# A hybrid decoder layer on one core: two lower bounds on GpSimd, a later sum, and other banks round the first scores

## The chip, the core and the metric

The kernel runs on one core of a Trainium2 chip, in one launch. Its time is device microseconds. The engines have names that the profile uses too: PE is TensorE, which multiplies matrices, and PEld is its loading of weights; DVE is VectorE, ACT is ScalarE, POOL is GpSimd, SP is SyncE, which issues most of the DMAs. Tiles of 128 partitions lie in SBUF; PE writes its results to PSUM, which the kernel uses as eight banks of 128x512 fp32.

## The reference, cut to what matters

One layer of a decoder over 1024 tokens of width 1024, all in float32:

```python
u = rms_norm(x, norm1_g)
aq, ak, av, hq, hf, hi, hg = split(u @ w_in)              # seven parts of 512 columns
attn = rms_norm(dilated_attention(aq, ak, av), attn_norm_g)   # 8 heads, windows (128,1) (512,4) (2048,16)
rec = hgrn2_mixer(hq, hf, hi, lb)                             # 4 heads, chunks of 64
rec = rms_norm(rec, hgrn_norm_g) * silu(hg)
h = x + concat(attn, rec) @ w_out
gate, val = split(rms_norm(h, norm2_g) @ w_up)
h = h + (gelu(conv3(gate)) * val) @ w_down
out = rms_norm(h, final_norm_g)

def hgrn2_mixer(q, f, i, lb):
    qf = silu(q)
    forget = lb + (1 - lb) * sigmoid(f)
    ...
```

So the recurrent part needs three kinds of sigmoid: of `hf` for the forget gate, and of `hq` and `hg` for the two silus.

## The kernel before, in words

A projection is done for a pair of 512-column parts at a time, by a scheme of seven products of 2x2 blocks in place of eight (`pair_block`, L527 on). Each operand is split into a high and a low part, so that one 128x128 by 128x512 step of a product is three matmuls (`three`, L514, L515, L516), and a product is four such steps. In a profile row `w<-T2h,whi` is such a matmul: `w` is the PSUM bank of the product, `T2h` the high part of a sum of token blocks, `whi` and `wlo` the parts of a weight block. Weights arrive by SP's DMAs as `raww`, are combined by DVE (L178, L179, L180, L197), cast to `whi` by ACT (L102), and the rest `wlo` is made by DVE (L104). DVE adds the products up out of PSUM (L544 to L556); only the first product of a block is copied out by ACT (L542).

The eight banks are handed out by name: `bank(tag, name)` has the tags "mm", "o", "t" and "s" with two banks each, in turn. Whoever asks for a bank whose turn has come waits until the last reader of its former contents is done. `block_banks[0]` says which tags the products of the next blocks take.

PE's order is written by hand: the program's order of matmuls is the order on PE. Long work (the products of the blocks) is a generator, `fill`, of which a stretch is run between other steps; `fill.run(x)` issues products for about x us. The order on DVE, ACT, POOL and SP is made by a scheduler from the program, so that an edit at one place can move their instructions elsewhere.

The stages that matter here:

- The first block of queries and keys runs before attention begins. After it `block_banks[0]` becomes `cycle(("mm",))` (L733), so that the blocks 1 to 3 take the two "mm" banks in turn, `fill.run(3.9)` issues the first products, and attention begins.
- Attention (L770 to L805) makes for each pair p of heads and block b of queries the scores of two heads into two banks (L788, L790; tags "s","s" for even b, "s","o" for odd b), takes them with mask and minimum to SBUF on DVE (L797), then exp on ACT (L799), reciprocal on DVE (L800), scaling on POOL (L801). Later PE transposes them (L816, L824; tag "t").
- The recurrence and its projections run from about 262 to 470 us. The projected parts are scaled on DVE (L951), bounded from below by -40 and sent through a sigmoid of three ACT instructions (L859, L860, L861): `f_out` (max in L915) for `hf`, `q_out` (L921, product L923) for `hq`, `g_last` (L928, product L930) for `hg`. The generator `recur` (L1015 on) then makes, per head and half of the tokens: two ACT instructions (L1020, L1021), a scan on DVE (L1027), differences and exponentials (L1031 to L1038), transposes on PE (`psK`, L1044), intra-chunk products (`psA`, L1049, L1050), chunk states (`psU`, L1060; L1062 to L1072 on DVE and ACT), a carry copied by POOL (L1075), outputs (`psO`, L1083, L1085, L1092), transposes of these (`psT`, L1098, tag "t"), and the gated result into `G` by DVE (L1100), which sets the "t" bank free.
- Within this stage `attn_stat` (one for each half of the tokens) makes the attention norm's statistic: four loads, squares on ACT (L968), additions on DVE (L970), and, as its second step, a sum over partitions by a matmul with ones into a "t" bank (`ass`, L973) with what follows from it (`rstd_part`, L369 to L373).

When each step of this stage comes is set by a list of times in units of 5.2 us of fill work: `STARTS` and `STAGES_AT` for the recurrence, `STAT = (3.5, 6.8)` plus 0 and 4.0 for the two steps of the statistic. `play` sorts the list and runs `fill` between the steps.

Of the kernel before, what the change touches and what calls it, by code (L numbers as in the profile page):

```python
# [3 lines left out]

# [31 lines left out]
STAT = (3.5, 6.8)  # L36
# [228 lines left out]
def hybrid_kernel(ctx: ExitStack, tc: tile.TileContext, xT, w_qk, w_tok, w_hg, w_out, w_up,  # L265
                  w_down, vecs, amask, hmask, out):
    nc = tc.nc
    PE, DVE, ACT, POOL = nc.tensor, nc.vector, nc.scalar, nc.gpsimd
# [132 lines left out]
    def bank(tag, name):  # L401
        return ps1.tile([P, H2], F32, tag=tag, name=name, bufs=2)
# [19 lines left out]
    def vtile(name):  # L422
        return at.tile([P, H2], F32, tag="vi", name=name, bufs=4)
# [135 lines left out]
    blocks, block_banks = [], [cycle(("mm",))]  # L559
# [136 lines left out]
    for t in TURN:  # L696
        x = vtile(f"it{t}")
        tok_out(ivd, t, x, V[t])

    def run(g):  # L700
        for _ in g:
            pass
# [18 lines left out]
    def qk_block(p):  # L721
        return pair_block(("qk", p), lambda m, hf: mtile(f"u{p}_{m}{hf}"), qk_evac(p))
# [7 lines left out]
    for hf in range(2):  # L730
        rms1_row(hf)
    run(first)
    block_banks[0] = cycle(("mm",))  # L733
    fill.add(*[qk_block(p) for p in range(1, 4)])
    fill.run(3.9)
    xp_cm.__exit__(None, None, None)
# [5 lines left out]
    if True:  # L742
# [29 lines left out]
        def scores(p, b):  # L772

            qp, kp = qk[p]
            far = 32 * max(b - 1, 0)
            near = P if b == 0 else 2 * P
            k0 = (b + 1) * P - near
            n = far + near
            S = [bank(("so" if b % 2 else "ss")[e], f"S{p}_{b}_{e}") for e in range(2)]
            rows = [slice(64 * e, 64 * e + 64) for e in range(2)]  # L780
            k4 = kp.rearrange("p (b r l) -> p r b l", r=4, l=32)
            for part in range(2 if far else 1):
                for r in range(4):
                    o = slice(32 * r, 32 * r + 32)
                    for e in range(2):
                        q = qp[rows[e], b * P + 32 * r : b * P + 32 * r + 32]
                        if part == 0:
                            PE.matmul(S[e][o, far:n], q, kp[rows[e], k0 : k0 + near], start=True, stop=True)  # L788
                        else:
                            PE.matmul(S[e][o, 0:far].rearrange("p (b l) -> p b l", l=32), q,  # L790
                                      k4[rows[e], r, 0 : b - 1], start=True, stop=True)
            m = mask[:, FAR - far :] if b else mask[:, FAR + P :]
            Ps = probs[p, b] = []
            for e in range(2):
                Pt = ab.tile([P, FAR + NEAR], F32, tag=f"P{e}", name=f"P{p}_{b}_{e}", bufs=3)
                st = at.tile([P, 16], F32, tag="st", name=f"st{p}_{b}_{e}", bufs=8)
                DVE.tensor_tensor_reduce(Pt[:, :n], S[e][:, :n], m, -(DH ** -0.5), BIG * 3,  # L797
                                         op0=ALU.add, op1=ALU.min, accum_out=st[:, 0:1])
                ACT.activation(Pt[:, :n], Pt[:, :n], AF.Exp, bias=st[:, 0:1], scale=-1.0, accum_out=st[:, 2:3])  # L799
                DVE.reciprocal(st[:, 3:4], st[:, 2:3])  # L800
                POOL.tensor_scalar(Pt[:, :n], Pt[:, :n], st[:, 3:4], 1.0, op0=ALU.mult, op1=ALU.mult)  # L801
                Ps.append(Pt)
# [55 lines left out]
        def sigmoid(dst, src):  # L858
            ACT.activation(dst, src, AF.Exp, scale=-1.0)  # L859
            ACT.activation(dst, dst, AF.Ln, bias=1.0)  # L860
            ACT.activation(dst, dst, AF.Exp, scale=-1.0)  # L861
# [17 lines left out]
        for x in slots[:LAG]:  # L879
            scores(*x)  # L880
            fill.run(1.5)
        ends = []
        for n, (p, b) in enumerate(slots):
            if n + LAG < len(slots):
                scores(*slots[n + LAG])
            if b == 0:
                for kb in range(2):
                    load_values(p, kb)
            fill.run((1.0 if ends else 2.5) if n < 22 else (0.8 if ends else 1.8))
            while ends:  # L890
                values(*ends.pop())
            turn(p, b)
            if b % 4 == 3:
                ends.append((p, b // 4))
# [6 lines left out]
    with pool("hg", "right") as hg:  # L901
# [3 lines left out]
        def ht(tag, nm, bufs=1):  # L905
            return hg.tile([P, H2], F32, tag=tag, name=nm, bufs=bufs)
# [3 lines left out]
        def tile_of(kind, h, hf):  # L910
            tag, bufs = {"hf": ("A", 4), "hq": ("E", 5), "hg": ("GH"[h // 2], 4)}[kind]
            return ht(tag, f"{tag}{h}_{hf}", bufs)
# [5 lines left out]

        def q_out(h, hf, E):
            F = ht("F", f"F{h}_{hf}")  # L920
            DVE.tensor_scalar_max(F, E, -40.0)  # L921
            sigmoid(F, F)
            DVE.tensor_mul(E, E, F)  # L923
            gate.setdefault((h, hf), {}).update(E=E)

        def g_last(h, hf, g_):
            F = ht("F", f"Fg{h}_{hf}")
            DVE.tensor_scalar_max(F, g_, -40.0)  # L928
            sigmoid(F, F)
            DVE.tensor_mul(g_, g_, F)  # L930
            G[h, hf] = g_
# [3 lines left out]
        def g_out(h, hf, g_):  # L935
            if (h, hf) in ready:
                g_last(h, hf, g_)
            else:
                waiting[h, hf] = g_

        def g_now(h, hf):
            ready.add((h, hf))
            if (h, hf) in waiting:
                g_last(h, hf, waiting.pop((h, hf)))

        OUT = {"hf": f_out, "hq": q_out, "hg": g_out}

        def hg_block(pair):
# [14 lines left out]
        def attn_stat(hf):  # L963
            acc = ht("H", f"asq{hf}", 4)
            for c in range(4):
                x = ar[c % 2]
                nc.sync.dma_start(x, rawd[c, hf])
                ACT.activation(x if c else acc, x, AF.Square)  # L968
                if c:
                    DVE.tensor_add(acc, acc, x)  # L970
            yield
            ss = bank("t", f"ass{hf}")
            PE.matmul(ss, ones, acc, start=True, stop=True)  # L973
            R2.append(rstd_part(ht("R", f"R2_{hf}", 2), acc, ss, 1.0 / 512))
            yield

        def attn_parts(hf):
            hi, lo = spare(f"attn{hf}")
            for c in range(4):
                a = ring.raw(rawd[c, hf])  # L980
                DVE.scalar_tensor_tensor(a, a, col(V_AG + c), R2[hf], op0=ALU.mult, op1=ALU.mult)
                ACT.copy(hi[:, c], a)
                DVE.tensor_sub(lo[:, c], a, f32(hi[:, c]))
            return hi, lo
# [16 lines left out]
        for hf in range(2):  # L1001
            for kind, h in HG[0]:
                x = tile_of(kind, h, hf)
# [121 lines left out]
        steps = []  # L1125
# [16 lines left out]
            steps += zip((start, *(start + x for x in STAGES_AT)), rec_steps(h, hf))  # L1142
        for hf in range(2):
            stat = attn_stat(hf)
            steps += [(STAT[hf] + x, lambda stat=stat: next(stat, None)) for x in (0, 4.0)]
            steps.append((PARTS[hf], lambda hf=hf: attn_ops.update({hf: attn_parts(hf)})))
        steps.sort(key=lambda x: x[0])
        done = 0
# [548 lines left out]
```

## Time and profile before

| | |
|---|---|
| median of 3 runs | 1142.49 us (1142.37 to 1142.78) |
| profiled execution, its time | 1142.57 us |
| its span, first to last instruction | 1140.6 us |
| mean granted TensorE clock | 0.998 |
| DVE, ACT, POOL busy | 85%, 51%, 8% of the span |
| PE busy from 268 to 316 us | 47.09 of 48 us |
| DVE busy from 268 to 316 us | 44.99 of 48 us |
| DVE busy from 390 to 470 us | 60.93 of 80 us |

A row of a timeline gives the start in us from the span's beginning, the duration in us, engine, line and operation, out<-in by the program's names, shapes, and the number of instructions put together; in brackets stands the time for which the engine was idle just before, and what ended that. Durations of neighbours on one engine overlap, so that the step from start to start is shorter than a duration. In a row of groups the count is followed by busy time in us, the mean in ns, and the idle time ahead of them with its releasers. In the view of waits a row is: who waited, for which producer, us in total, times, the longest. A row of windows has the busy time of each engine in a stretch, with the number of instructions in brackets.

### The profile page before, as it was taken

The page shows a single profiled execution, that of the slowest core. Times are in us where ns is not written, and L with a number is a line of the kernel's source. Part 1 is how long each engine was busy: PE and PEld are TensorE (multiplying, and loading weights), DVE is VectorE, ACT ScalarE, POOL GpSimd, SP SyncE. Part 2 cuts the span into 40 slices and gives each one's busy share as a digit, 9 for nine tenths or more (in the row PEclk, how much of TensorE's full clock was granted, in tenths as well). Part 3 has the DMA queues.
Part 4 walks back from the last instruction along what each step waited for, and adds up shares of the span by engine and source line. Part 5 has one row for each costly group of instructions (what it writes and reads, how often), then busy time and mean ns, then how long its engine had stood idle before and what let it go on. Part 6 is the DMA issues. An engine that isn't in the chain of part 4 may idle for free.

```text
span 1140.6 us, 17940 instructions
## 1 busy us (share of the span) xinstructions
PE 1127.5 (99%) x6404; PEld 927.4 (81%) x6404; DVE 970.2 (85%) x1768; ACT 580.6 (51%) x1151; POOL 89.9 (8%) x107
## 2 busy tenths in 40 slices
PE   9999999999999999999999999999999999999996
PEld 8888677778878888888788888888888888888885
DVE  7687977778999985989999999888988789857987
ACT  7545545465788665564433434343434444444553
POOL 5200333330000002000000000000000000000000
PEclk9999999999999999999999999999999999999999
DMA  7147322224315542311233223322332376435532
GB/s 251 64 169 235 73 71 62 85 76 159 102 57 179 168 139 92 104 50 56 65 121 111 92 103 120 117 79 100 120 117 79 134 263 219 120 94 176 157 120 74
DMA packets 102088, 136.13 MB, mean 119 GB/s; under 512 B 25392, under 2 KB 44624, under 8 KB 102000
## 3 DMA queue, kind: packets, MB, share of 16 engines
q1 hardware_dynamic: 87712, 110.33, 31.6%
q10 hardware_dynamic: 14288, 24.67, 5.8%
q8 instruction: 50, 0.82, 0.3%
q14 instruction: 38, 0.31, 0.1%
HBM read 100.20 MB, written 34.76 MB: 118 GB/s over the span
## 4 chain that ended last, share of the span: by engine, by line
PE 93%; DVE 5%; DMA 1%; issue 1%; ACT 0%; DVEq 0%; ACTq 0%
PE p L1298 11%; PE p L1297 11%; PE p L1296 11%; PE w L514 5%; PE w L515 4%; PE w L516 4%; PE ds L1595 3%; PE ds L1597 3%; PE ds L1596 3%; PE po L514 3%; PE po L516 3%; PE po L515 3%; PE da L1597 2%; PE da L1595 2%; PE da L1596 2%; PE S L788 2%
## 5 line engine op out<-in xcount | busy, mean ns | idle before, releaser
L102 ACT CAST whi<-raww 128x512 fp32r<-128x512 f32 x253 | 154.5, 618 | 209.3 <-PE p L1297 75.4
L104 DVE TENSOR_TENSOR wlo<-raww,whi 128x512 fp32r<-128x512 f32 x254 | 176.9, 699 | 23.1 <-ACT whi L102 21.5
L102 ACT CAST whi<-r 128x512 fp32r<-128x512 f32 x70 | 43.6, 623 | 82.6 <-PE ds L1596 46.2
L104 DVE TENSOR_TENSOR wlo<-r,whi 128x512 fp32r<-128x512 f32 x70 | 48.0, 687 | 18.9 <-ACT whi L102 18.9
L1596 PE MATMUL ds<-flo,whi 128*128 128x512 f32 x160 | 62.3, 389 | 0.0
L1595 PE MATMUL ds<-fhi,whi 128*128 128x512 f32 x160 | 62.2, 389 | 0.0
L1296 PE MATMUL p<-b1h,whi 128*128 128x512 f32 x160 | 62.2, 389 | 0.0
L1297 PE MATMUL p<-b1l,whi 128*128 128x512 f32 x160 | 62.2, 389 | 0.0
L1298 PE MATMUL p<-b1h,wlo 128*128 128x512 f32 x160 | 62.2, 389 | 0.0
L1597 PE MATMUL ds<-fhi,wlo 128*128 128x512 f32 x160 | 62.2, 389 | 0.0
L801 POOL TENSOR_SCALAR P<-P,st 128x128 f32<-128x128 f32 (+7 forms) x64 | 47.1, 742 | 97.2 <-DVE st L800 77.1
L1569 POOL TENSOR_TENSOR facc<-facc,sqf 128x256 f32<-128x256 f32 x2 | 1.5, 735 | 670.9 <-ACT sqf L1568 670.9
L104 DVE TENSOR_TENSOR flo<-rawf,fhi 128x512 fp32r<-128x512 f32 x70 | 48.1, 687 | 4.0 <-ACT fhi L102 4.0
L102 ACT CAST fhi<-rawf 128x512 fp32r<-128x512 f32 x70 | 43.1, 616 | 13.2 <-PE p L1298 5.0
L1325 ACT ACTIVATE cv<-cv 128x512 f32<-128x512 f32 x44 | 27.8, 633 | 41.6 <-DVE cv L1318 41.6
L799 ACT ACTIVATE P<-P,st 128x128 f32<-128x128 f32 (+7 forms) x64 | 35.7, 559 | 25.6 <-DVE st L797 25.6
L1318 DVE SCALAR_TENSOR_TENSOR cv<-g,vec,cv 128x511 f32<-128x511 f32 (+2 forms) x92 | 44.8, 492 | 3.4 <-ACT cv L1315 3.1
L1595 PE MATMUL da<-fhi,whi 128*128 128x512 f32 x120 | 46.7, 389 | 0.0
L1596 PE MATMUL da<-flo,whi 128*128 128x512 f32 x120 | 46.7, 389 | 0.0
L1597 PE MATMUL da<-fhi,wlo 128*128 128x512 f32 x120 | 46.7, 389 | 0.0
L797 DVE CUSTOM_DVE_ANT_0 P<-S,mask 128x128 f32<-128x128 f32 (+7 forms) x64 | 28.8, 486 | 8.7 <-PE S L790 6.6
L1597 PEld LDWEIGHTS ds<-fhi,wlo 128*128 128x128 f32 x160 | 30.0, 188 | 6.3
(589 smaller groups left out, 3411.3 us busy)
## 6 DMA issues: line engine op xcount, KB each, us to landing
raww<-in_w_up_dram SPq DMA_DIRECT2D x88, 256.0 KB, 2.9
rawf<-spT SPq DMA_DIRECT2D x40, 256.0 KB, 2.8
r<-in_w_down_dram SPq DMA_DIRECT2D x40, 256.0 KB, 3.5
spB<-a ACTq DMA_DIRECT2D x30, 256.0 KB, 2.2
spT<-t ACTq DMA_DIRECT2D x30, 256.0 KB, 2.1
rawf<-spB SPq DMA_DIRECT2D x30, 256.0 KB, 2.8
raww<-in_w_out_dram SPq DMA_DIRECT2D x28, 256.0 KB, 2.8
raww<-in_w_hg_dram SPq DMA_DIRECT2D x24, 256.0 KB, 2.8
```

Of the source, the lines that this page charges most:

```text
L102: self.pin(self.high(hi[:, :w], raw))
L104: self.pin(low.tensor_sub(lo[:, :w], raw, f32(hi[:, :w])))
L514: PE.matmul(ps, a[0], b[0], start=start, stop=False)
L515: PE.matmul(ps, a[0], b[1], start=False, stop=False)
L516: PE.matmul(ps, a[1], b[0], start=False, stop=stop)
L801: POOL.tensor_scalar(Pt[:, :n], Pt[:, :n], st[:, 3:4], 1.0, op0=ALU.mult, op1=ALU.mult)
L1296: PE.matmul(ps, hi[:, s], bhi, start=(start and n == 0), stop=False)
L1297: PE.matmul(ps, hi[:, s], blo, start=False, stop=False)
L1298: PE.matmul(ps, lo[:, s], bhi, start=False, stop=(stop and n == len(rhs) - 1))
L1595: PE.matmul(ps[d], hi[:, s], ahi, start=(k == 0), stop=False)
L1596: PE.matmul(ps[d], hi[:, s], alo, start=False, stop=False)
L1597: PE.matmul(ps[d], lo[:, s], ahi, start=False, stop=(k == NPAIR - 1))
```

## The change

Four edits:

1. The first two products of the second query and key block take the two "t" banks, those behind them "mm" in turn as before.
2. The scores of pair 0, block 0, take the tags "s" and "t" in place of "s" and "s".
3. The max with -40 in `q_out` and in `g_last` is issued on POOL in place of DVE: six and eight instructions of 128x512. That of `f_out` stays on DVE.
4. The second step of `attn_stat` is asked for at +4.3 in place of +4.0 units, that is 0.3 x 5.2 = 1.56 us of fill work later, in both halves.

```diff
-from itertools import cycle
+from itertools import chain, cycle
...
     run(first)
-    block_banks[0] = cycle(("mm",))
+    block_banks[0] = chain(('t', 't'), cycle(("mm",)))
     fill.add(*[qk_block(p) for p in range(1, 4)])
     fill.run(3.9)
...
-            S = [bank(("so" if b % 2 else "ss")[e], f"S{p}_{b}_{e}") for e in range(2)]
+            S = [bank(("so" if b % 2 else "ss" if (p, b) != (0, 0) else 'st')[e], f"S{p}_{b}_{e}") for e in range(2)]
...
         def q_out(h, hf, E):
             F = ht("F", f"F{h}_{hf}")
-            DVE.tensor_scalar_max(F, E, -40.0)
+            POOL.tensor_scalar_max(F, E, -40.0)
             sigmoid(F, F)
             DVE.tensor_mul(E, E, F)
...
         def g_last(h, hf, g_):
             F = ht("F", f"Fg{h}_{hf}")
-            DVE.tensor_scalar_max(F, g_, -40.0)
+            POOL.tensor_scalar_max(F, g_, -40.0)
             sigmoid(F, F)
             DVE.tensor_mul(g_, g_, F)
...
             stat = attn_stat(hf)
-            steps += [(STAT[hf] + x, lambda stat=stat: next(stat, None)) for x in (0, 4.0)]
+            steps += [(STAT[hf] + x, lambda stat=stat: next(stat, None)) for x in (0, 4.3)]
```

What it does to the order is shown at three places; in these rows a number behind a name tells one tile from the next of that name, and + is the kernel with the change.

First, DVE at the first scores: `S_0_0`, `S_0_1` are the two heads' scores of block 0, `S_1_0` the first of block 1, `u_01` the block's sum.

```order
 L197 TENSOR_TENSOR raww_1111<-raww_1111,raww_1057 128x512
 L544 TENSOR_TENSOR u_01_1178<-u_00_1159,w_1179 128x512
+L104 TENSOR_TENSOR wlo_1245<-raww_1111,whi_1244 128x512
 L797 ISA P_0_0_1228,st_0_0_1229<-S_0_0_1218,mask 128x128
 L797 ISA st_0_0_1229 128x1
 L797 ISA P_0_1_1234,st_0_1_1235<-S_0_1_1219,mask 128x128
 L797 ISA st_0_1_1235 128x1
-L104 TENSOR_TENSOR wlo_1245<-raww_1111,whi_1244 128x512
-L800 RECIPROCAL st_0_0_1229<-st_0_0_1229 128x1
-L800 RECIPROCAL st_0_1_1235<-st_0_1_1235 128x1
 L797 ISA P_1_0_1263,st_1_0_1264<-S_1_0_1253,mask 128x256
```

The rest of a weight block, L104, now stands ahead of the scores' first two reads, and the two reciprocals between them and block 1's read stand behind it. PE's order is the same here as before.

Second, PE at the first statistic's sum, taken from the place where it stood to the one where it stands.

```order
 L516 MATMUL w_3862<-T2h,wlo_3699 128x512
 L1060 MATMUL psU_1_3866<-iv_1_3642,kT_1_3790 128x128 x3
-L973 MATMUL ass_3880<-asq_3573,ones 128x512
 L514 MATMUL w_3862<-T2h,whi_3698 128x512
 L515 MATMUL w_3862<-T2l,whi_3698 128x512
```

```order
 L515 MATMUL w_3862<-T2l,whi_3698 128x512
 L516 MATMUL w_3862<-T2h,wlo_3699 128x512
+L973 MATMUL ass_3902<-asq_3573,ones 128x512
 L514 MATMUL w_3862<-T2h,whi_3698 128x512
 L515 MATMUL w_3862<-T2l,whi_3698 128x512
```

It stands two steps of a product, six matmuls, later. On DVE the instruction that sets its bank free, L1100, stands in these rows:

```order
 L104 TENSOR_TENSOR wlo_3827<-raww_3694,whi_3826 128x512
-L923 TENSOR_TENSOR E_1_3703<-E_1_3703,F_1_3753 128x512
 L556 TENSOR_TENSOR A_1_3599<-w_3801,A_1_3599 128x512
-L921 TENSOR_SCALAR F_0_3795<-E_0_3680 128x512
+L1100 SCALAR_TENSOR_TENSOR G_0_3387<-psT_0_3844,vec,G_0_3387 128x512
 L951 TENSOR_TENSOR A_1_3599<-A_1_3599,R_90 128x512
-L1100 SCALAR_TENSOR_TENSOR G_0_3387<-psT_0_3844,vec,G_0_3387 128x512
+L1027 SCALAR_TENSOR_TENSOR C_0_3885<-chunks,A_0_3551 128x512
+L923 TENSOR_TENSOR E_0_3680<-E_0_3680,F_0_3795 128x512
 L915 TENSOR_SCALAR A_1_3599<-A_1_3599 128x512
```

L1100 has moved ahead of one L951. The scan L1027, which stood just ahead of the first of these rows before, stands behind it. A max of `q_out` is gone from between; one L923 has moved a few rows up, and a few rows ahead of all these an L197 is new that stood behind L1100 before.

Third, ACT at the first max that is now on POOL: `Fg_0` is its result, the input of the first sigmoid of `g_last`.

```order
 L102 CAST whi_3445<-raww_3439 128x512
 L1021 ACTIVATE A_0_3372<-A_0_3372,lb 128x512
+L859 ACTIVATE Fg_0_3714<-Fg_0_3714 128x512
 L1033 ACTIVATE ex_0_3466<-C_0_3464 128x4
 L1034 ACTIVATE ex_0_3466<-C_0_3464 128x4
 L102 CAST whi_3485<-raww_3439 128x512
+L860 ACTIVATE Fg_0_3714<-Fg_0_3714 128x512
 L1032 ACTIVATE ex_0_3466<-A_0_3372 128x4
```

The three instructions of this sigmoid stood about 25 places further back; two of them are now ahead of the recurrence's exponentials and of a weight cast.

## The prediction

> **What bounds the kernel now.** I read the page first, then what PE waited for, then PE's timeline at each of these waits, and last the timelines of VectorE (DVE), ScalarE (ACT) and GpSimd (POOL) round the same moments. The first two rows are the head of the page and its list of busy times.
>
> ```profile
> span 1140.6 us, 17940 instructions
> ...
> PE 1127.5 (99%) x6404; PEld 927.4 (81%) x6404; DVE 970.2 (85%) x1768; ACT 580.6 (51%) x1151; POOL 89.9 (8%) x107
> ```
>
> TensorE is busy 1127.5 of 1140.6 us, so PE's idle time is the whole stock from which a change of waits can draw: 13.1 us. The view of PE's waits says how little of it lies in the middle.
>
> ```profile
> PE warm L433 <- DVE eps L295: 1.1, 1, 1.1
> PE w L514 <- ACT u L542: 1.0, 1, 1.0
> PE ass L973 <- DVE G L1100: 0.9, 1, 0.9
> PE S L788 <- DVE st L797: 0.5, 1, 0.5
> ```
>
> The first is the start, which the diff doesn't touch. The other three, each met once, sum to 2.4 us; the remaining 9.6 us are start and tail, untouched too. Each of the three belongs to an edit: `w` to the new banks of the block, `S` to the bank of the first scores, `ass` to the later sum. The gain is thus a little under 3 us at the most. A difference of 0.2%, 2.28 us, is about what a measurement of this kernel can tell from no change, so full success is just over that bound and two thirds of it is not.
>
> **Edit 1, banks of the block.** PE's timeline at the first wait:
>
> ```profile
> 117.53 0.39 PE L516 MATMUL w<-B11h,wlo 128*128 128x512 f32 x1
> 118.93 0.50 PE L514 MATMUL w<-T2h,whi 128*128 128x512 f32 x1 [1.01 <-ACT u L542]
> 119.26 0.40 PE L515 MATMUL w<-T2l,whi 128*128 128x512 f32 x1
> 119.50 0.39 PE L516 MATMUL w<-T2h,wlo 128*128 128x512 f32 x1
> ```
>
> The second product of the block (T2) reuses the "mm" bank of the first, which ACT has copied out when PE goes on at 118.93. From start to start that is 1.40 us where the last two rows step by 0.24: 1.16 too many; and the step behind it, 0.33, is 0.09 too long: **1.25 us**. With a "t" bank for each of the two, the wait for that copy is gone. The copy now stands in the way of whoever takes the first bank next, the second half of scores (0,0), which edit 2 gives a "t" bank. By the order PE gets there after nine matmuls of T2, 9 x 0.24 = 2.2 us from 117.77: at 119.9, 1.0 us after the copy's end. So nothing is passed on, and the term lies between 1.0 (the wait alone) and 1.25.
>
> **Edit 2, bank of the first scores.** PE at the second wait, and the next scores, which do not wait:
>
> ```profile
> 122.83 0.40 PE L516 MATMUL w<-B21h,wlo 128*128 128x512 f32 x1
> 123.68 0.67 PE L788 MATMUL S<-kp,qp 64*32 64x256 f32 x16 [0.46 <-DVE st L797]
> ...
> 125.54 0.40 PE L516 MATMUL w<-B21h,wlo 128*128 128x512 f32 x1
> 125.87 0.66 PE L788 MATMUL S<-kp,qp 64*32 64x256 f32 x16
> ```
>
> Scores take 0.85 us after a matmul in the first case and 0.33 in the second: **0.52 us**. Late next are the third scores, (0,2), which need both "s" banks: one is free early, the other must be read by L797 of (0,1). DVE now:
>
> ```profile
> 122.64 0.69 DVE L544 TENSOR_TENSOR u<-u,w 128x512 f32<-128x512 f32 x1 [0.56 <-PE w L516]
> 123.24 0.28 DVE L797 CUSTOM_DVE_ANT_0 P<-S,mask 128x128 f32<-128x128 f32 x1
> ...
> 124.56 0.41 DVE L797 CUSTOM_DVE_ANT_0 P<-S,mask 128x256 f32<-128x256 f32 x1
> ```
>
> L544 waited 0.56 us, so DVE's L197 ahead of it was done at 122.08; its product comes 1.25 us earlier now, so it follows L197 at once. The new order puts L104 ahead of the scores' L797. L104's weight cast on ACT needs L197's result, so it begins at 122.08 too and lasts as long as L104 or a little less, by estimate 0.65 with the handing over: L104 starts near 122.75, and L797 of (0,0) 0.60 later (as from 122.64 to 123.24), near 123.35. With two of these at 0.2 (0.28 less the overlap of rows, 122.64 + 0.69 - 123.24 = 0.09), the first of (0,1) begins at 123.75 and ends at 124.16. PE is at the third scores at 125.87 - 1.25 - 0.52 = 124.10. With a release of 0.1 it waits about **0.2 us**; nothing if the cast comes earlier, 0.5 to 0.7 if DVE is late by half an L104 or more.
>
> **Edit 4, the later sum.** PE at the third wait:
>
> ```profile
> 314.01 0.83 PE L1060 MATMUL psU<-iv,kT 128*128 128x128 f32 x6
> 315.75 1.13 PE L973 MATMUL ass<-asq,ones 128*128 128x512 f32 x2 [0.91 <-DVE G L1100]
> ```
>
> The sum's "t" bank was the last transposes', and L1100 reads it late. The wait is 0.91 us, and by the excess of the other two over their waits (1.25 against 1.01, 0.52 against 0.46) it costs 0.97 to 1.15: I take **1.1 us**. PE now does six more matmuls first, 6 x 0.24 = 1.4 us, so it is at the sum at 314.84 + 1.4 = 316.2 where before it was at 314.84 (315.75 less 0.91). DVE is read in the rows behind this paragraph. By the last of them L1100 in the old pace ends at 315.69, half a microsecond before that. Both engines come earlier by the first two terms: DVE waited for PE at the first of these rows and moves with it until then.
>
> ```profile
> 274.52 0.69 DVE L545 TENSOR_TENSOR G<-w,G 128x512 f32<-128x512 f32 x1 [0.72 <-PE w L516]
> ...
> 276.40 1.22 DVE L1027 TENSOR_TENSOR_SCAN C<-chunks,A 128x512 f32<-128x512 f32 x1
> ...
> 278.72 0.69 DVE L548 TENSOR_TENSOR G<-w,G 128x512 f32<-128x512 f32 x1
> ...
> 314.95 0.74 DVE L1100 SCALAR_TENSOR_TENSOR G<-psT,vec,G 128x512 f32<-128x512 f32 x1
> ```
>
> By the order of the changed kernel L1100 also stands ahead of the next scan (1.22 less the overlap, 1.13) and of one L951 (0.6, as any of this size), and behind one L197 (0.6) more. With the three maxes that leave DVE ahead of it (0.34 each, next paragraph) DVE has 1.13 + 0.6 - 0.6 + 1.0 = 2.1 us less to do before it. The cover is 0.5 + 2.1 = 2.6 us. The statistic's later readers cost nothing: the second sum stands six matmuls later as well, and PE doesn't wait there now. The sum's loads and squares stay at their step; no DMA is moved.
>
> **Edit 3, two kinds of max on POOL.** The groups of DVE, in the window from 262 to 462 us, that leave it (14 in all, four more read `H`), and in the next fence the nearest thing that POOL does:
>
> ```profile
> L921 DVE TENSOR_SCALAR F<-E 128x512 f32<-128x512 f32 x6 | 2.5, 418 | 0.0
> L928 DVE TENSOR_SCALAR Fg<-G 128x512 f32<-128x512 f32 x4 | 1.7, 422 | 0.0
> ```
>
> ```profile
> L801 POOL TENSOR_SCALAR P<-P,st 128x448 f32<-128x448 f32 x8 | 6.4, 801 | 9.3 <-DVE st L800 9.3
> ```
>
> DVE steps about 0.34 us at such a max (0.42 less the overlap): 14 x 0.34 = 4.8 us less on DVE. POOL has room: its own time, by estimate at most 0.8 x 512/448 = 0.9 us each, waits included, falls into a stage where it does next to nothing (a row under the rivals). What isn't free is how the two engines get at memory. The carry's copy on POOL, in a full and in a quiet stretch of DVE, then the DVE row at which the first one got through, and one of DVE from the kernel's start:
>
> ```profile
> 298.86 2.76 POOL L1075 COPY carry<-U 128x128 f32<-128x128 f32 x1 [42.68 <-PE w L516]
> ```
>
> ```profile
> 408.08 0.29 POOL L1075 COPY carry<-U 128x128 f32<-128x128 f32 x1 [18.79 <-DVE U L1071]
> ```
>
> ```profile
> 301.39 0.68 DVE L548 TENSOR_TENSOR E<-w,A 128x512 f32<-128x512 f32 x1
> ```
>
> ```profile
> 23.12 1.78 DVE L104 TENSOR_TENSOR wlo<-raww,whi 128x512 fp32r<-128x512 f32 x1
> ```
>
> The same copy takes 0.29 us in the quiet and 2.76 while DVE runs back to back on SBUF tiles; it ends at 301.62, 0.23 us after DVE begins L548, which reads a bank of PSUM. Conversely, that L104, between POOL's long additions at the start, takes 1.78 us, not the 0.69 of the other DVE rows of this size. So a max on POOL waits for a gap, up to 2.5 us, and its user on ACT waits with it; DVE's price per max lies between -0.34 (nothing held) and 1.78 - 0.69 - 0.34 = +0.75 us. I take the end near -0.34, since POOL got in beside L548 there, and that L548 kept its 0.68. The Trainium skill ("SBUF — State Buffer", section "Who interferes with whom") says that a GpSimd instruction reading SBUF and a DVE instruction with two SBUF inputs lock each other out for whole instructions, the first issued winning; the copy's 2.76 against 0.29 agrees. By that rule a lucky order costs DVE nothing and an unlucky one a max's length each, which is the slower rival below.
>
> The added wait matters where something is queued behind it. ACT now has the first sigmoid of `Fg0_0` ahead of this row:
>
> ```profile
> 277.66 0.21 ACT L1033 ACTIVATE ex<-C 128x4 f32<-128x4 f32 x1 [1.78 <-DVE C L1027]
> ```
>
> The max's input is ready as the scan of 276.40 begins. If it gets in at once it ends near 277.3 and the sigmoid (0.6) ends before 277.9, 0.2 late. If it waits for the first DVE instruction that reads PSUM, the L548 of 278.72 above, it ends near 279.4, and ACT is 2.3 us late. Behind it stand a weight cast and the recurrence's exponentials, for which DVE's L104 and L1037, L1038 wait, for these PE:
>
> ```profile
> 281.14 0.68 DVE L1038 TENSOR_TENSOR B<-B,A 128x512 f32<-128x512 f32 x1
> ```
>
> ```profile
> 285.89 0.60 PE L1044 MATMUL psK<-ident,B 128*128 128x128 f32 x4
> ```
>
> PE has 285.89 - 281.82 = 4.1 us of cover there, and the sum above 2.6. Without that cover the hold would cost its 2.3 us whole. So edit 3 by itself is **0** for PE, whose waits in the stage are none but `ass`; its relief of DVE is of use to the sum alone.
>
> **The sum.** 1.25 + 0.52 - 0.2 + 1.1 = 2.7 us. The profiled execution took 1142.57 us (span 1140.6 and 2.0 around it), 0.1 above the median of 1142.49; 1142.57 - 2.7 = 1139.9, and I give that for the median too.
>
> **Rivals.** *The sum still waits.* POOL's waits make L1100 late by more than the cover: a hold of 2.3 us, and three maxes that hold DVE by 0.1 or more each. For it: DVE in the stage that follows is as full as this row shows (columns PE, PEld, DVE, ACT, POOL busy, clock, DMA share, GB/s).
>
> ```profile
> 316.00:390.00 74.00, 74.00 (x404) 61.32 (x404) 73.20 (x136) 59.17 (x143) 2.08 (x2) 1.00 0.42 129
> ```
>
> Against it: that the order takes 2.1 us out ahead of L1100. It keeps 0.5 to 0.9 of the 1.1: 1140.6.
>
> *The score stall only moves.* The third scores wait 0.5 to 0.7, since the cast ahead of L104 is later than I have it: 1140.3. For it: the cast's 0.65 is an estimate, and PE is there 0.1 us ahead of its bank as it is. Against it: every step of DVE there is counted with the new order's instructions, and L197, on which the cast hangs, had no wait of its own to move.
>
> *Slower.* POOL's maxes hold DVE as in the row of 23.12. Ten of the fourteen, the groups quoted, stand before 390 us, where DVE has 0.8 us of idle in 74. At +0.75 each, 7.5 us, and with ACT's 2.3, DVE is 9.8 us late; PE's cover of 4.1 is used up and 5.7 us come out as waits at the recurrence's matmuls: 1139.9 + 5.7 = 1145.6. It decides as soon as DVE's lateness passes 4 us, about five maxes in. Against it: a max is one pass of 0.6 to 0.9 us, not POOL's train of long additions, and most gaps are at instructions that read PSUM.
>
> *The change does not do what it says.* The block's new banks could free nothing if the scores then waited for them; the order shows the bank of each, and it has 1.1 us of room. More than 2.9 us would need a wait elsewhere to go.
>
> **How the numbers follow.** Forecast 0.58 (1139.3 to 1140.2), the sum still waits 0.17, the scores' stall moves 0.12, slower 0.07, both middle rivals or little gain 0.04, more gain 0.02. The first ends at 1140.2, which is the bound for faster: 0.60 with the last. The two middle rivals and the mixed case end between 1140.3 and 1142: 0.33 within 0.2%. The range, 1139.3 to 1142.0, leaves out the slower rival and the two fringes.
>
> **What would show it.** In the profile after, PE's view of waits should have lost L514 behind L542 and L973 behind L1100, and may have a new S L788 behind L797 of about 0.2. POOL's L921 and L928 should last 0.6 to 2.8 us each, and DVE's rows next to them should keep their 0.68 (1.3 or more would be the slower rival). L1100 should end before PE reaches the sum. The prediction is wrong if PE shows a wait at psK, psU or psT between 268 and 390 us, or if a wait appears at a place that I have not named.

## The result, and the profile after

| | before | after |
|---|---|---|
| median | 1142.67 us (1142.37 to 1142.86, 5 runs) | 1150.38 us (1148.71 to 1151.33, 5 runs) |
| ratio, 95% interval | | 1.0065 (1.0055 to 1.0076) |
| profiled execution, span | 1142.57, 1140.6 us | 1150.2, 1148.4 us |

The kernel became slower by 0.65%, 7.7 us, where 2.7 us of gain were forecast. The head of the page of the changed kernel and its view of PE's waits:

```profile
span 1148.4 us, 17955 instructions
...
PE 1130.7 (98%) x6404; PEld 928.7 (81%) x6404; DVE 969.2 (84%) x1754; ACT 579.7 (50%) x1151; POOL 112.6 (10%) x121
```

```profile
PE po L514 <- DVE h L1191: 3.2, 1, 3.2
PE w L514 <- DVE A L544: 1.4, 1, 1.4
PE psO L1085 <- ACT st L1072: 1.3, 3, 0.6
PE psT L1098 <- DVE on L1092: 1.1, 2, 0.6
PE warm L433 <- DVE eps L295: 1.0, 1, 1.0
```

The three waits of before are all gone, and 7.0 us of others stand in their place. PE's busy time also rose by 3.2 us for the same 6404 matmuls. Where each lies is told by the starts of the same PE instruction in both traces:

| PE instruction | before | after | difference |
|---|---|---|---|
| first product, at the start | 6.74 | 7.23 | +0.49 |
| first T2 matmul of the block | 118.93 | 118.17 | -0.76 |
| scores (0,1) | 123.68 | 122.27 | -1.41 |
| L515 of the T2 product behind the first sum | 318.33 | 315.75 | -2.58 |
| psO, second half's carry | 346.39 | 346.61 | +0.22 |
| first T1 matmul, L514 | 350.70 | 352.67 | +1.97 |
| psT | 378.25 | 381.13 | +2.88 |
| first po matmul of attn1 | 397.19 | 403.45 | +6.26 |
| the seventh behind it | 398.80 | 406.61 | +7.81 |

The gains came as forecast, and more: 1.25 and 0.65 at the first two places, then 1.17, 3.1 us in all by 318 us. Behind that 10.4 us are lost until 407 us, and nothing more to the end. PE's timeline of the changed kernel at the block's banks, at the scores and at the sum, which answer to the three stalls of before:

```profile
117.95 0.39 PE L516 MATMUL w<-B11h,wlo 128*128 128x512 f32 x1
118.17 0.39 PE L514 MATMUL w<-T2h,whi 128*128 128x512 f32 x1
...
121.94 0.40 PE L516 MATMUL w<-B21h,wlo 128*128 128x512 f32 x1
122.27 0.66 PE L788 MATMUL S<-kp,qp 64*32 64x256 f32 x16
...
124.12 0.40 PE L516 MATMUL w<-B21h,wlo 128*128 128x512 f32 x1
124.45 0.45 PE L788 MATMUL S<-kp,qp 64*32 64x256 f32 x8
```

```profile
314.42 0.40 PE L516 MATMUL w<-T2h,wlo 128*128 128x512 f32 x1
314.66 1.02 PE L973 MATMUL ass<-asq,ones 128*128 128x512 f32 x2
```

None of the three waits: T2 starts 0.22 us behind the matmul ahead of it, both scores 0.33, the sum 0.24. Then the loss. POOL's groups, and what ACT and DVE waited for from 268 to 412 us:

```profile
L921 POOL TENSOR_SCALAR F<-E 128x512 f32<-128x512 f32 x6 | 10.4, 1728 | 46.0 <-DVE E L951 20.1 <-ACT A L861 12.2 <-DVE hss L373 7.8
L928 POOL TENSOR_SCALAR Fg<-H 128x512 f32<-128x512 f32 x4 | 8.2, 2052 | 20.0 <-DVE H L930 10.5 <-DVE hss L373 9.5
...
L928 POOL TENSOR_SCALAR Fg<-G 128x512 f32<-128x512 f32 x4 | 6.9, 1725 | 29.5 <-DMA raww<-in_w_hg_dram 20.5 <-DVE E L923 8.9
```

```profile
ACT Fg L859 <- POOL Fg L928: 13.1, 6, 3.6
ACT F L859 <- POOL F L921: 11.9, 6, 3.8
```

```profile
DVE wlo L104 <- ACT whi L102: 6.4, 5, 2.6
DVE E L923 <- ACT F L861: 4.6, 5, 1.3
```

On the mean of a group a max lasts 1.7 to 2.1 us on POOL (single ones 1.48 to 3.00) where it lasted 0.42 on DVE, and ACT stood still for POOL twelve times, 25.0 us in all. Before, it had waited for these maxes on DVE six times, 7.7 us. What stands behind on ACT is late too, and so is DVE, which waited 11.0 us in these two rows: for the products behind the sigmoids (L923), and for weight casts that have nothing to do with a sigmoid but stand behind one on ACT (L104; 2.8 us there before).

The largest wait shows the whole chain. POOL, ACT, DVE and PE of the changed kernel, each from its timeline:

```profile
397.81 3.00 POOL L928 TENSOR_SCALAR Fg<-H 128x512 f32<-128x512 f32 x1 [3.01 <-DVE H L930]
```

```profile
400.84 0.63 ACT L859 ACTIVATE Fg<-Fg 128x512 f32<-128x512 f32 x1 [3.62 <-POOL Fg L928]
401.38 0.19 ACT L370 ACTIVATE hss<-hss 128x4 f32<-128x4 f32 x1
401.47 0.60 ACT L102 CAST whi<-raww 128x512 fp32r<-128x512 f32 x1
```

```profile
397.57 1.29 DVE L1111 TENSOR_TENSOR rec0l<-G,rec0h 128x512 fp32r<-128x512 f32 x2
398.78 0.69 DVE L1111 TENSOR_TENSOR rec1l<-G,rec1h 128x512 fp32r<-128x512 f32 x1
402.11 0.69 DVE L104 TENSOR_TENSOR wlo<-raww,whi 128x512 fp32r<-128x512 f32 x1 [2.64 <-ACT whi L102]
402.71 0.68 DVE L1191 TENSOR_TENSOR h<-po,xr 128x512 f32<-128x512 f32 x1
```

```profile
403.45 0.79 PE L514 MATMUL po<-attn1h,whi 128*128 128x512 f32 x1 [3.19 <-DVE h L1191]
404.05 0.63 PE L515 MATMUL po<-attn1l,whi 128*128 128x512 f32 x1
404.47 0.63 PE L516 MATMUL po<-attn1h,wlo 128*128 128x512 f32 x1
```

The max, issued while DVE runs three L1111 on SBUF tiles, takes 3.00 us. ACT waits 3.62 us for it with a weight cast two rows behind, DVE 2.64 for that cast, and PE 3.19 for L1191, which stands on DVE behind L104 and empties PE's bank. The weight cast, L104, L1191 and the matmul all wait in line behind the sigmoid, and none of them uses its result.

### The profile page after: what moved, and what is told of

It reads as the page before. It is cut to its first block, busy times and chain, and to the rows that moved or that the text cites. A ratio compares the mean times of both kernels' runs of the same rounds, so it can differ in the third digit from the quotient of the medians.

```text
span 1148.4 us, 17955 instructions
## 1 busy us (share of the span) xinstructions
PE 1130.7 (98%) x6404; PEld 928.7 (81%) x6404; DVE 969.2 (84%) x1754; ACT 579.7 (50%) x1151; POOL 112.6 (10%) x121
## 4 chain that ended last, share of the span: by engine, by line
PE 89%; DVE 5%; ACT 2%; POOL 1%; issue 1%; DMA 0%; SPq 0%; DVEq 0%; POOLq 0%
PE p L1298 11%; PE p L1296 11%; PE p L1297 11%; PE w L514 5%; PE w L516 4%; PE w L515 4%; PE ds L1597 3%; PE ds L1596 3%; PE ds L1595 3%; PE po L514 2%; PE da L1597 2%; PE da L1596 2%; PE da L1595 2%; PE po L516 2%; PE po L515 2%; PE S L788 2%
## 5 line engine op out<-in xcount | busy, mean ns | idle before, releaser
L104 DVE TENSOR_TENSOR wlo<-raww,whi 128x512 fp32r<-128x512 f32 x254 | 178.1, 704 | 27.7 <-ACT whi L102 26.1
L104 DVE TENSOR_TENSOR wlo<-r,whi 128x512 fp32r<-128x512 f32 x70 | 48.1, 688 | 19.5 <-ACT whi L102 18.6
L801 POOL TENSOR_SCALAR P<-P,st 128x128 f32<-128x128 f32 (+7 forms) x64 | 46.3, 728 | 95.6 <-DVE st L800 90.3
L104 DVE TENSOR_TENSOR flo<-rawf,fhi 128x512 fp32r<-128x512 f32 x70 | 48.0, 686 | 3.7 <-ACT fhi L102 3.7
L1596 PEld LDWEIGHTS ds<-flo,whi 128*128 128x128 f32 x160 | 30.0, 188 | 6.3
L1298 PEld LDWEIGHTS p<-b1h,wlo 128*128 128x128 f32 x160 | 30.0, 188 | 6.3
```

Of the source, the lines that this page charges most:

```text
L104: self.pin(low.tensor_sub(lo[:, :w], raw, f32(hi[:, :w])))
L1298: PE.matmul(ps, lo[:, s], bhi, start=False, stop=(stop and n == len(rhs) - 1))
L1596: PE.matmul(ps[d], hi[:, s], alo, start=False, stop=False)
```

## The experiments

Three theories stood against each other. *Latency*: a max lasts so much longer on POOL that ACT, which takes its instructions in order, waits for it, and DVE for ACT. *Ports*: POOL and DVE stop each other at SBUF, as the slower rival had it. *Order*: the rearranged rows on DVE and ACT are late by themselves. All times are medians; the kernel before had 1142.5 to 1142.9 us beside them.

**Which edit.** Edit 3 left out (`no_pool`), and edit 3 alone (`pool_only`):

```diff
-            POOL.tensor_scalar_max(F, E, -40.0)
+            DVE.tensor_scalar_max(F, E, -40.0)
...
-            POOL.tensor_scalar_max(F, g_, -40.0)
+            DVE.tensor_scalar_max(F, g_, -40.0)
```

> Edits 1, 2 and 4 without the maxes on POOL. In the trace of the change PE's starts gained 1.25 us at the block's banks, 0.66 at the scores and 1.2 at the sum against the kernel before, and lost some 10.5 us behind those, so far put down to the maxes. Theory 'latency' (a max on POOL lasts 1.5 to 3 us, ACT waits for it in order, DVE for ACT) and theory 'ports' (POOL and DVE stop each other at SBUF) both expect 1139.3 to 1140.0 us here and no PE wait behind 130 us. Theory 'order' (the edits' rearranging of DVE and ACT makes the waits, whoever runs the max) expects more than 1143.

Measured: 1140.56 us (1140.24 to 1141.32), ratio 0.9981 (0.9972 to 0.9990). The loss is gone; that leaves out theory *order* as it was put. But the time is 0.6 above what was expected, and PE does wait behind 130 us (the traced execution took 1141.32 us, the longest of the eleven):

```profile
PE w L514 <- DVE A L544: 0.8, 1, 0.8
PE ass L973 <- DVE G L1100: 0.3, 1, 0.3
```

> Edit 3 alone on the kernel before. Theories 'latency' and 'ports' expect the loss whole: 1142.6 + 10.5 = 1153 us, a little less if the statistic's sum hides some of it, 1150 to 1154. Theory 'order' (all edits together) expects 1142 to 1146.

```diff
-            DVE.tensor_scalar_max(F, E, -40.0)
+            POOL.tensor_scalar_max(F, E, -40.0)
...
-            DVE.tensor_scalar_max(F, g_, -40.0)
+            POOL.tensor_scalar_max(F, g_, -40.0)
```

Measured: 1152.58 us (1151.64 to 1153.06), ratio 1.0085 (1.0071 to 1.0099). Edit 3 by itself costs 9.9 us.

**How long the max is, and whom it holds.** A small kernel with POOL and DVE alone:

```python
for _ in range(4): POOL.tensor_scalar_max(a, a, -40.0)                                    # L78, nothing beside it
...
for _ in range(4): POOL.tensor_scalar(a, a, st[:, 3:4], 1.0, op0=ALU.mult, op1=ALU.mult)  # L82
...
for _ in range(4): POOL.tensor_scalar_mul(a, a, 1.0)                                      # L88
...
POOL.tensor_copy(e, a)                                                                    # L90
...
for _ in range(14): DVE.tensor_add(c, c, d)     # L101, both inputs in SBUF; beside it four maxes, L103
...
for _ in range(14): DVE.tensor_add(c, c, w)     # L110, w in PSUM; beside it four maxes, L112
```

> Only a few instructions: POOL's max of 128x512 alone, four times in a row, and other forms of the same size; then DVE additions on SBUF tiles back to back with four maxes beside them, the same with one input in PSUM, and with one in three so. The rest of the layer is left out. Theory 'latency' expects a lone max of about 1.5 us (the shortest in the trace of the change was 1.48) and DVE additions that keep their step of 0.60 beside it. Theory 'ports' expects a lone max of 0.6 to 0.9 us, and additions on SBUF that step by 1.1 or more beside it.

Its POOL and DVE timelines (L80 is the max with a multiplication behind it in one instruction):

```profile
3.38 6.19 POOL L78 TENSOR_SCALAR a<-a 128x512 f32<-128x512 f32 x4 [2.96 <-DMA a<-in_xT_dram]
9.65 7.93 POOL L80 TENSOR_SCALAR a<-a 128x512 f32<-128x512 f32 x4
17.68 3.05 POOL L82 TENSOR_SCALAR a<-a,st 128x512 f32<-128x512 f32 x4
...
31.60 6.20 POOL L88 TENSOR_SCALAR a<-a 128x512 f32<-128x512 f32 x4
37.86 0.61 POOL L90 COPY e<-a 128x512 f32<-128x512 f32 x1
44.37 7.21 POOL L103 TENSOR_SCALAR f<-f 128x512 f32<-128x512 f32 x4 [5.90 <-DVE c L99]
57.93 6.18 POOL L112 TENSOR_SCALAR g<-g 128x512 f32<-128x512 f32 x4 [6.36 <-DVE c L108]
```

```profile
44.32 11.29 DVE L101 TENSOR_TENSOR c<-c,d 128x512 f32<-128x512 f32 x14
...
57.88 10.07 DVE L110 TENSOR_TENSOR c<-c,w 128x512 f32<-128x512 f32 x14
```

A lone max lasts 6.19/4 = 1.55 us, 3.7 times the 0.42 that it took on DVE in the kernel before. The form of instruction from which the prediction sized it, L801's two multiplications, takes 3.05/4 = 0.76 on a tile of the same size, so columns alone don't give the price. Nor is the max dear as such: one multiplication by a number, L88, also lasts 1.55. What in the form makes the difference, these rows don't say. Beside additions on SBUF a max lasts 1.80 and DVE loses (11.29 - 10.07)/4 = 0.3 us per max; beside additions with an input in PSUM neither loses anything (with one in three so, a max lasts 1.64). Theory *latency* had the max right; its step of 0.60 for DVE's additions was not met, since these step by 0.72 where nothing is lost and by 0.81 beside the maxes on SBUF. Theory *ports* missed both: it had 0.6 to 0.9 for the lone max and 1.1 or more for the step. So the ports are real, but not as dear for DVE as 0.75 us a max. For POOL they can be: the max of 3.00 us above, beside three L1111 with their inputs in SBUF, is 1.45 us longer than a lone one.

**The same order, another length.** Here only POOL's operation is another; the rows on DVE and ACT are those of the change.

```diff
-            POOL.tensor_scalar_max(F, E, -40.0)
+            POOL.tensor_copy(F, E)
```

and the same for `g_` (`copy_len`), or

```diff
-            POOL.tensor_scalar_max(F, E, -40.0)
+            POOL.tensor_scalar(F, E, -40.0, 1.0, op0=ALU.max, op1=ALU.mult)
```

(`slow_len`).

> The whole change, with POOL's 14 maxes replaced by copies of the same tiles: the lower bound is left out, the order on DVE and ACT is that of the change, row for row. A lone POOL copy took 0.61 us beside 1.55 for the lone max. Theory 'latency': each max on the path is 0.94 shorter, and with 7 to 10 of them on the path 6.5 to 9.5 of the 10.5 us come back: 1141 to 1144 us. Theory 'ports': at most what DVE lost beside the maxes in the small kernel, (11.29 - 10.07)/4 = 0.3 us each, 14 x 0.3 = 4.2 us: 1146 or more. Theory 'order' (these rows in this order are late whatever the max lasts): 1150.

Measured: 1141.53 us (1140.94 to 1142.02), ratio 0.9990 (0.9981 to 0.9999).

> The whole change, with the max followed by a multiplication by one in the same POOL instruction: 1.98 us alone in place of 1.55, the same order on DVE and ACT, and the same result. Theory 'latency': 7 to 10 times 0.43 more, 1153 to 1155 us. Theory 'ports': as many accesses as before, within 1 us of 1150.4. Theory 'order': 1150.4.

Measured: 1154.83 us (1154.42 to 1154.95), ratio 1.0105 (1.0089 to 1.0122).

In this table the last column is the median and the others are from the traces: the operation's mean in the kernel, ACT's waits for POOL, DVE's waits in the two rows L104 and L923 shown above, and PE's waits behind the start.

| POOL's operation | alone | in the kernel | ACT | DVE | PE | the whole kernel |
|---|---|---|---|---|---|---|
| copy | 0.61 us | 1.05 us | 15.2 us | 5.6 us | 1.6 us | 1141.53 us |
| max (the change) | 1.55 us | 1.82 us | 25.0 us | 11.0 us | 7.0 us | 1150.38 us |
| max and multiplication | 1.98 us | 2.25 us | 27.7 us | 14.5 us | 10.1 us | 1154.83 us |

The time follows the length: 8.85 us for 0.94, 4.45 for 0.43, 9.4 and 10.3 times the difference, as if about ten of the fourteen lay on the path one behind the other. Both times lie where theory *latency* expected them; theories *ports* and *order* both miss both numbers. The waits of DVE and PE grow with it, and PE's waits together with its busy time (1127.5, 1130.7 and 1132.2 us) come to 8.6 and 4.6 us for the two steps. DVE's busy time, which the ports would stretch, hardly does, and not at all over the second step: it is 966.1 us where neither engine has the maxes (the run without them, below), 967.7 with the copy, 969.2 with the max and 969.0 with the longest. In the copy's trace one wait is left of the chain at 397 us:

```profile
PE po L514 <- DVE h L1191: 1.4, 1, 1.4
PE warm L433 <- DVE eps L295: 1.1, 1, 1.1
PE w L514 <- DVE A L544: 0.2, 1, 0.2
```

**Which of the two kinds.** Edits 1, 2, 4 with only one of edit 3's two lines.

> Edits 1, 2, 4 and only q_out's six maxes on POOL. q_out's product L923 was what DVE waited for in the trace of the change (4.6 us before L923, none before L930). Theory 'latency' expects most of the loss here, 1145 to 1149. Theory 'ports' expects 6/14 of it: 1144 to 1145.

Measured: 1143.08 us (1142.52 to 1144.39), ratio 1.0005 (0.9996 to 1.0015).

> Edits 1, 2, 4 and only g_last's eight maxes on POOL. Theory 'latency' expects the smaller part, 1141 to 1144: the gate is wanted much later than the max, and the harm is ACT's wait ahead of other work. Theory 'ports' expects 8/14 of it: 1146 to 1147.

Measured: 1144.39 us (1144.15 to 1146.01), ratio 1.0017 (1.0007 to 1.0026).

Both missed, by either theory: `q_out`'s part is less than expected, and `g_last`'s more than 'latency' and less than 'ports' expected of it. Against edits 1, 2 and 4 they cost 2.5 and 3.8 us, 6.3 together, where both at once cost 9.8. `g_last` by itself already brings PE's wait for L1191 (2.5 us), and about 1.5 us of slower matmuls behind it (last section); ACT waits 11.9 us for POOL in its trace, whatever the sigmoid is wanted for. That each alone costs less than its share would follow if each uses up cover that the other then lacks; no run tells that from another cause, and how the loss divides among the single maxes stays open.

**What the relief of DVE is worth, and what became of edit 4.** The 14 maxes left out altogether:

```diff
-            POOL.tensor_scalar_max(F, E, -40.0)
-            sigmoid(F, F)
+            sigmoid(F, E)
```

and the same in `g_last`.

> Edits 1, 2 and 4, and the 14 maxes left out on both engines, so that these sigmoids have no lower bound: what DVE's relief of 14 x 0.34 = 4.8 us is worth by itself. Theory 'latency' and theory 'ports' expect PE without a wait behind 130 us and so the time of the edits 1, 2 and 4 alone within 0.3 us, 1139.3 to 1140.0. If it is faster by 0.5 us or more, PE is held by DVE at places that the view of waits doesn't show.

Measured: 1139.46 us (1139.34 to 1139.80), ratio 0.9972 (0.9961 to 0.9982). It is in the expected band, but not within 0.3 us of edits 1, 2 and 4: it is 1.1 below them, because those did worse than expected. PE's waits for `ass` and for L544 are gone in its trace. So DVE's relief is worth 1.1 us beside edits 1, 2 and 4, and with POOL's max it was not to be had; a better place of the sums, below, comes within 0.3 us of it with the maxes on DVE (1139.73). Then the banks alone, and edit 4 alone:

> Edits 1 and 2 alone. Their terms as the trace of the change showed them, 1.25 and 0.66 us, with no new score wait: 1142.5 - 1.9 = 1140.6 us, the sum's wait of 0.9 still there. If the edits' gains add up plainly, edits 1, 2 and 4 together (1140.56) would then have got nothing out of edit 4.

Measured: 1140.90 us (1140.34 to 1142.06), ratio 0.9984 (0.9975 to 0.9992). It is 0.3 us above the expected time, and as much above edits 1, 2 and 4, which is less than the spread of either; its trace still has the sum's wait, 0.6 us.

> Edit 4 alone. The theory that it moves the wait (with the sum later, the statistic's L372 and L373 of the second half stand ahead of L544 on a full DVE, and PE waits 0.8 us for L544's bank at 350 us) expects 1142.0 to 1142.6. The prediction's 1.1 us of gain would be 1141.4.

Measured: 1142.59 us (1142.03 to 1143.37), ratio 0.9998 (0.9990 to 1.0007). Edit 4 alone gains nothing that can be measured; its trace has lost the wait for `ass` and got one of 0.4 us for L544. The last two kernels place the sums otherwise, with edits 1 and 2 and the maxes on DVE:

```diff
-            steps += [(STAT[hf] + x, lambda stat=stat: next(stat, None)) for x in (0, 4.3)]
+            steps += [(STAT[hf] + x, lambda stat=stat: next(stat, None)) for x in (0, 4.0 if hf else 4.3)]
```

and, in the second, 4.6 in place of 4.3.

> Edits 1, 2, and edit 4 for the first half of the tokens only. If the second sum's place makes the wait for L544 at 350 us, that wait is gone and the time is 0.6 to 1.0 us below edits 1, 2 and 4: 1139.6 to 1140.0. If DVE is late there whatever stands in what order, 1140.5.

Measured: 1139.73 us (1139.50 to 1140.01), ratio 0.9973 (0.9962 to 0.9983). Its view of PE's waits holds the start alone:

```profile
PE warm L433 <- DVE eps L295: 1.1, 1, 1.1
```

So the second sum's later place made the wait for L544. By what step is told by DVE's rows before the change and with edits 1, 2 and 4:

```profile
344.36 1.45 DVE L981 SCALAR_TENSOR_TENSOR raww<-raww,vec,R 128x512 f32<-128x512 f32 x2
...
348.13 0.68 DVE L373 SCALAR_TENSOR_TENSOR R<-asq,R 128x512 f32<-128x512 f32 x1
...
349.33 0.67 DVE L544 TENSOR_TENSOR A<-A,w 128x512 f32<-128x512 f32 x1
349.93 0.74 DVE L981 SCALAR_TENSOR_TENSOR raww<-raww,vec,R 128x512 f32<-128x512 f32 x1
```

```profile
343.76 0.79 DVE L981 SCALAR_TENSOR_TENSOR raww<-raww,vec,R 128x512 f32<-128x512 f32 x1
...
345.07 0.74 DVE L981 SCALAR_TENSOR_TENSOR raww<-raww,vec,R 128x512 f32<-128x512 f32 x1
...
346.34 0.74 DVE L981 SCALAR_TENSOR_TENSOR raww<-raww,vec,R 128x512 f32<-128x512 f32 x1
...
348.20 0.68 DVE L373 SCALAR_TENSOR_TENSOR R<-asq,R 128x512 f32<-128x512 f32 x1
348.80 0.68 DVE L544 TENSOR_TENSOR A<-A,w 128x512 f32<-128x512 f32 x1
```

The statistic's L372 and L373 stand ahead of L544 in both, so that they, to which the expectation of `sum_only` put the wait, are not what is new. New is the third L981 ahead of it, 0.67 us. In `sum_only` it stands there too; with the second sum left where it was, it stands behind L544 again, and in the next kernel as well. With only the first sum moved the kernel leaves nothing of the computation out, and is 3.2 us below the kernel before beside it (1142.93) and 10.7 below the change.

> Edits 1, 2 and the sums at +4.6 units in place of +4.3. In its order L544 stands ahead of L372 and L373 again, and the first sum is six matmuls later still: both of PE's new waits (0.8 for L544, 0.3 for the sum) should go, 1139.3 to 1139.8 us, level with the kernel without the maxes, 1139.46. If DVE is late there whatever the order, 1140.3 to 1140.6.

Measured: 1140.36 us (1140.10 to 1141.89), ratio 0.9981 (0.9972 to 0.9990). The two waits are gone as expected, but two others have come (PE for `psT` behind DVE's L1092, 0.6 us), and the expected time is missed: it lies where DVE was expected to be late whatever the order.

## Why the prediction was wrong

**Edits 1 and 2: right.** 1.25 us was forecast for the block's banks and 1.25 was measured. For the scores I took 0.52 and a new wait of 0.2; it was 0.65 with no new wait, so that rival didn't come. The banks alone gave 2.0 us.

**Edit 4: right at its place, not in what it is worth.** 1.1 us was forecast, 1.17 came at that place in the trace of the change, and the sum no longer waited. What the prediction lacked: it took the second sum as free, because PE had no wait there. On a DVE that was busy 73.20 of 74 us a third L981 then stands ahead of L544, and PE waits for its bank. Alone the edit is worth nothing; with the second sum left where it was, it is worth 1.2 us (1140.90 against 1139.73).

**Edit 3: the step that failed.** It reads: "its own time, by estimate at most 0.8 x 512/448 = 0.9 us each, waits included", and, from it, "edit 3 by itself is 0 for PE". A lone max is 1.55 us and those in the kernel 1.82 on the mean. The estimate scaled another operation by its columns, and took it as an upper bound, though POOL's additions of 128x512 with two inputs lasted 1.33 us on the mean in the trace before (L1206). That is the term of the sum that was mis-sized: 0 in the forecast, 9.9 us in the run of edit 3 alone. The single maxes, 1.48 to 3.00 us, all but one lie within the 0.6 to 2.8 that the prediction named as a sign; its sum allowed for such a wait at one place, and for none at the others.

How the wait was counted is the smaller part. "Its user on ACT waits with it" was written, and worked out once, for the first max, as 2.3 us against a cover of 4.1. There it held: PE's first wait is not at the first max but behind the fourth, at 321 us. ACT then waited twelve times, 25.0 us. But how often it waits does not decide. The copies, with 1.05 us in the kernel, are about as long as the estimate had the maxes, and ACT waits for them twelve times too, 15.2 us; yet that kernel is only 1.0 us above edits 1, 2 and 4. So of the 9.8 us that edit 3 cost beside the others, about 8.8 hang on the length, and about 1 would have been missed with a max of the length that was estimated.

**The slower rival** had a chance of 0.07 and a time of 1145.6. Its direction was right and its mechanism not: it had DVE held by 0.75 us a max, where 0.3 was measured in the small kernel. The Trainium skill ("SBUF — State Buffer", section "Who interferes with whom") is borne out by the small kernel in which instructions get in each other's way: 1.80 us and 0.3 us beside inputs in SBUF, 1.55 and nothing beside one in PSUM. That one holds the other for its whole length, as the prediction took from it, is not borne out: one behind the other, 14 additions and four maxes would take 10.07 + 6.19 = 16.3 us, and the additions were through in 11.29. Another page of the Trainium skill ("GPSIMD Engine Reference", section "4.1 Engine selection") puts elementwise max on VectorE, and calls GpSimd roughly line-rate for one input. The first half is what the runs say; for the second the copy comes near, 0.61, and the max doesn't, 1.55 against DVE's 0.42.

**What would show it wrong** was named: PE waiting at psT, and waits at places not named. Both came.

## What to carry to other kernels

Price an operation on another engine from the same operation there, not from one of like shape; where the trace has none, the bound is open upwards. When work leaves a full engine for a slow one, ask who waits in order for its result, what stands behind that waiter, and from what length on it shows: here fourteen copies cost about 1 us, fourteen maxes, 0.94 us longer each, 8.9 us more, while the relief was worth 1.1 us at the most. A wait that goes at a full engine can come back at another bank, so move one thing and look again: the fastest kernel here that leaves nothing out has the two bank edits and only one of the two sums moved.

## What the runs showed of the hardware that was not expected

After the longest of PE's waits the granted clock fell. These windows of the changed kernel stand ahead of, in and behind it (columns as in the row of windows above: busy PE, PEld, DVE, ACT, POOL, then the clock):

```profile
399.00:403.40 4.40, 1.26 (x11) 0.61 (x7) 1.76 (x5) 2.56 (x7) 1.81 (x1) 0.98 0.06 21
403.40:406.60 3.20, 3.15 (x7) 2.48 (x8) 3.15 (x7) 1.78 (x4) 1.48 (x1) 0.50 0.72 229
406.60:410.00 3.40, 3.40 (x18) 2.82 (x17) 2.94 (x4) 2.95 (x7) 0.25 (x1) 1.00 0.30 95
```

At a clock of 0.50 the seven matmuls from 403.45 step by 0.43 us (the first by 0.60) in place of 0.23, so the wait of 3.19 us cost 1.55 us more behind its end (from +6.26 to +7.81 in the table of starts). With only `g_last` on POOL, PE waited 2.52 us for the same L1191; there the first matmuls behind it stepped by 0.23 us, and those from 399.19 to 402.18 by 0.43 (clock 0.60 from 398.7 to 403.0). Behind the copy's wait of 1.41 us, at the same place, the clock stayed at 1.00. The runs don't say where between the two the change lies, or whether it is the wait alone that decides.

On POOL the operations of one kind of instruction differ by a factor of 2.6: 0.76 us for two multiplications of 128x512 with a factor from a tile, 1.55 for one multiplication by a number and for one max, 1.98 for a max and a multiplication.
